# A two-product feed-forward kernel with an order written by hand: high and low parts placed as steps of their own, the written order carried on to the middle of the second product, and four row blocks made in the last unit

## The chip, the cores and the metric

One Trainium2 chip; the program runs on one of its cores. The metric is the device time of one execution in microseconds (us), the median of several runs. The engines of the core are TensorE (PE; its weight loads are listed as PEld), VectorE (DVE), ScalarE (ACT), GpSimd (POOL) and SyncE (SP), which in this kernel issues most DMAs.

## What is computed

One layer of a hybrid trunk over 640 tokens (128 context tokens and 512 latent ones) at a width of 1024: one input projection feeds differential attention, a gated linear recurrence and grouped-query attention, whose outputs are joined and multiplied by `w_out`. A squared-ReLU MLP follows. Cut to the part that matters here, with `g1`, `sh2`, `sc2`, `g2` from the conditioning:

```python
x = LN1(alpha * x + g1 * (mixed @ w_out))          # 640 x 1024
h = x * (1 + sc2) + sh2                            # what the MLP reads
f = square(relu(h @ w_ff1)) @ w_ff2                # 1024 -> 4096 -> 1024
y = LN2(alpha * x + g2 * f)
```

Inputs and outputs are 32-bit floats.

## The kernel before

**Numbers as pairs.** Every large matmul takes its two operands split into a high and a low part. `split` (L90) does it: ScalarE copies the value into the rounded type (the high part, L91), then VectorE subtracts that from the value (the low part, L92). A product is three matmuls, high by high, high by low and low by high (`mm3`, L127, and `prod`, L1417). So an operand is ready only when ScalarE and then VectorE have done their step.

**The output projection** runs in two halves of 512 columns. In each, the five token tiles t (128 tokens) are multiplied in turn (`wo_gemm`, 24 matmuls a tile), VectorE adds the result to the stream (`residual`, L1217; it multiplies by the gate at L1226, which is the reader of the PSUM bank), and takes the statistics (`half_stats`, `norm_stats`). After the second half `normalize` (ScalarE, L1255 to L1258) finishes the tile, `turn` (TensorE, L1268) transposes it in two groups of four blocks, each group into a PSUM bank, and `h2` scales and shifts the group into the MLP's input: the first group by ScalarE (L1281), the second by VectorE (L1279). The input is kept as four quarters `raws[i, j]`: half j of the tokens by half i of the features.

**The first product** (h by `w_ff1`) is made by seven products instead of eight per 2 by 2 block, in 16 units u of 256 hidden columns, two row blocks each. The seven, with their operands, are m1 (a11, b11), m2 (a12, b21), m6 (s2, t2), m5 (s1, t1), m7 (s3, t3), m4 (a22, t4), m3 (s4, b22): 12 matmuls of 320 tokens each. a11, a12 and a22 are quarters of the input, s1 to s4 sums of quarters (`sums12` and its neighbours); the b are quarters of a unit's weights and the t their sums, made by VectorE (`b_sums`, L1300); `load` fetches a unit's weights, and `take` (L1316) splits them: 1 for b11, 2 for b21 and b22, 3 for the four t. In PSUM m1, m6, m7 and m4 add up in bank x, m2 stands in y, m5 and m3 add up in z. `keep` (ScalarE, L1431) copies bank x after m1, m6 and m7, because the next product adds to the same bank and so has to wait for that copy. c11, c22, c12 and c21 (VectorE L1439 to L1444, ScalarE L1436 and L1437) add bank and copy and square the result, and `store` writes a row block to memory through GpSimd's queue, or leaves it in `st` for the last two units. In units 8 to 11 a part of g2 is made as well: `gate2` (L1499) loads weights `wad` into the buffer of a unit's weights, and 8 small matmuls use each half of it at the unit's end.

**The second product** (by `w_ff2`) has two halves n of 512 columns. Its five accumulators take all 32 row blocks in pairs. The blocks of unit 14 come first (`first_pair`, `first_rows`, L1574 and L1620), from weights loaded and split inside the last unit. The loop from L1672 then fetches `wg_i` (512 KB for the blocks i and i+1, two buffers) and reads the stored row blocks `hidb`, splits both, and multiplies; a pair of row blocks is 30 matmuls. In the first half `alpha_rows` (L1655) stands at its tenth block: it loads the rows of LN1's scale and shift, multiplies them by alpha on ScalarE (L1660) and applies them to the stream on VectorE. `gate_rows` (L1207) spreads g2 by two matmuls into `psabg2x` and `psabg2y` (L1213), and ScalarE copies them (L1214).

**What sets the order.** Between `manual_schedule` (after the first half of the output projection) and `region.close()` (after `first_rows`), TensorE, ScalarE and VectorE carry out their instructions as the code writes them. Everything else is ordered by a scheduler. Each engine works through its queue in that order, so a step that waits holds up every step behind it on its engine.

Of the kernel before, what the change touches and what calls it, by code (L numbers as in the profile page):

```python
# [62 lines left out]
def hybrid_layer_kernel(ctx: ExitStack, tc: tile.TileContext, T):  # L63
# [1198 lines left out]
    def turn(t):  # L1262

        for q in range(2):
            pst[t, q] = ps_f(f"psh{t}{q}")
            for k in range(4):
                kk = q * 4 + k
                PE.transpose(pst[t, q][:, k * P : (k + 1) * P], xn[:, t, kk * P : (kk + 1) * P], ident)  # L1268

    def h2(t, q):  # L1270
# [3 lines left out]
        for o, n, th, c0 in spans:  # L1274
# [8 lines left out]
    def split_sum(n, src, lo=0, hi=HALF):  # L1283
        split(sums[n][0][:, :, lo:hi], sums[n][1][:, :, lo:hi], src[:, :, lo:hi])
# [29 lines left out]
    def take(u, what, lo=None, hi=None):  # L1314

        g, o = U[u], u % 2  # L1316
        names, off, src = {
            1: (("b11",), 0, lambda: g.r[:, 0:1, :, 0, :]),
            2: (("b21", "b22"), 2, lambda: g.r[:, 1].rearrange("p k c n -> p c k n")),
            3: (("t1", "t3", "t2", "t4"), 0, lambda: g.t),  # L1320
        }[what]
        lo, hi = lo or 0, hi or len(names)
        if what == 3:
            h, l = f3[o][0][:, lo:hi], f3[o][1][:, lo:hi]
        else:
            n = len(names)
            h, l = f12[o][:, off + lo : off + hi], f12[o][:, off + n + lo : off + n + hi]
        split(h, l, src()[:, lo:hi])
        for i in range(lo, hi):
            g.w[names[i]] = (h[:, i - lo], l[:, i - lo])  # L1330

# [12 lines left out]
    def wo_gemm(t, n, wk):  # L1344
        ps = ps_f(f"pswo{n}{t}")
# [3 lines left out]

    g1r = gate_rows("g1", 0)  # L1350
    wk = wo_weights(0)
    for t in range(NT):
# [16 lines left out]
    for t in range(NT):  # L1369
        ps = wo_gemm(t, 1, wk)  # L1370
        if t == 0:
            g1r = gate_rows("g1", 1)
        if 0 < t < 4:
            turn(t - 1)
        residual(t, 1, ps, g1r, ALPHA)
        half_stats(t, 1, "a")
        mvs[t] = norm_stats(t)
        if t == 4:
            break
        if t > 0:  # L1380
            h2(t - 1, 0)
            h2(t - 1, 1)
        normalize(t, mvs[t])
        if t == 1:
            f3[0] = [wop.tile([P, 4, 4, P], F32R, tag=tag, name=f"wf3{p}0") for p, tag in (("h", "wr"), ("l", "w3"))]
            take(0, 3)
        if t == 2:
            f12 = [mpool[0].tile([P, 6, 4, P], F32R, tag=f"mx{p}", name=f"wf12{p}") for p in "hl"]
            split_sum("a11", raws[0, 0], 0, 256)
            split_sum("a12", raws[0, 1], 0, 256)  # L1390
        if t == 3:
            split_sum("a12", raws[0, 1], 256)
# [22 lines left out]
    def banks(u):  # L1415
        U[u].ps = {b: fps[0].tile([P, 512], F32, tag=b, name=f"ps{b}{u}") for b in "xyz"}
# [96 lines left out]
    m1(0)  # L1513
    turn(3)
    m2(0)
    h2(3, 0)
    take(1, 1)
    h2(3, 1)
# [15 lines left out]
    take(1, 2, 1, 2)
    parts("s1")
    split_sum("s1", s1r)
    m6(1)
    keep(1, 2)
    load(2, wop, "w0")
# [15 lines left out]
    c11(0)  # L1555
    m4(0)
# [233 lines left out]
```

## Time and profile before

| | |
|---|---|
| three runs | 965.54, 967.46, 968.42 us; median 967.46 |
| the profiled execution | 969.56 us, its span 967.8 us |
| mean granted TensorE clock | 0.974 of full speed |
| busy: TensorE, VectorE, ScalarE, GpSimd | 885.0, 664.4, 473.8, 69.0 us |
| bytes moved | 109.19 MB, 113 GB/s over the span |

The profile is one execution. In a row of a timeline stand the start and the duration in us, the engine, the line of the kernel, the operation, what it writes and reads, the tile's shape and the number of instructions; in brackets how long the engine was idle ahead of it and what released it (`<-ACT a L91` means that it waited for the high part that line 91 writes). Matmuls are pipelined, so their starts are what to subtract. The row blocks of a trace's names appear as `hidb`, the parts of the input as `a` and `s`, the weights as `wf12`, `wf3` (their low parts end in l, except where both parts share a buffer), their raw form as `wf_r`, and the sums as `wf_t`.

### The profile page before, as it was taken

The numbers are of one execution on the slowest core, as the hardware profiler recorded it, in microseconds if no ns is written. First come the engines' busy times: TensorE is split into PE (matmuls) and PEld (weight loads), VectorE is DVE, ScalarE is ACT, GpSimd is POOL, SyncE is SP. The second block draws the span as 40 slices with busy tenths as digits, with TensorE's granted clock in tenths as the row PEclk, the third lists the DMA queues.
The fourth block names the chain that finished last, engine by engine and source line by source line (L and its number), as shares of the span: only waits on it lengthen the run. The fifth ranks groups of instructions, "written<-read, shape, count | busy, mean of one in ns | idle before, by whom it ended". The sixth has DMA issues, their size and how long they took to land.

```text
span 967.8 us, 15412 instructions
## 1 busy us (share of the span) xinstructions
PE 885.0 (91%) x5941; PEld 764.0 (79%) x5941; DVE 664.4 (69%) x1231; ACT 473.8 (49%) x972; POOL 69.0 (7%) x136
## 2 busy tenths in 40 slices
PE   6879889999999998999966799999995999999996
PEld 4778776889989776777766799888994888888885
DVE  2369997998786878866756777666754843474448
ACT  3567675476564658632643455444544433153320
POOL 2200010210100100010000000110000000000000
PEclk9999998999999999999979899999997999999998
DMA  9952615423031120053003344455406852052202
GB/s 259 281 154 66 188 37 159 113 83 93 18 99 43 54 90 1 2 204 122 1 1 100 128 142 142 143 172 189 146 28 232 300 175 87 23 174 69 83 11 99
DMA packets 102026, 109.19 MB, mean 113 GB/s; under 512 B 6688, under 2 KB 82176, under 8 KB 101952
## 3 DMA queue, kind: packets, MB, share of 16 engines
q1 hardware_dynamic: 95968, 91.67, 30.6%
q0 software_dynamic: 5792, 16.44, 4.9%
q8 instruction: 47, 0.77, 0.3%
q14 instruction: 27, 0.22, 0.1%
q10 hardware_dynamic: 192, 0.08, 0.0%
HBM read 95.59 MB, written 12.58 MB: 112 GB/s over the span
## 4 chain that ended last, share of the span: by engine, by line
PE 65%; DVE 14%; DMA 9%; ACT 7%; issue 3%; SPq 2%; DVEq 0%; ACTq 0%
PE psx L1425 9%; PE psy L129 7%; PE psy L130 7%; PE psy L131 7%; PE psz L1425 5%; DMA wad<-in_w_ada 3%; PE psA L130 2%; PE psA L129 2%; PE psA L131 2%; PE psavA L731 2%; DMA adaw<-in_w_ada 2%; PE psy L1425 2%; DMA wf_r<-in_w_ff 2%; PE psavC L953 1%; DVE b_st L561 1%
## 5 line engine op out<-in xcount | busy, mean ns | idle before, releaser
L92 DVE TENSOR_TENSOR gl<-hidb,gh 128x640 fp32r<-128x640 f32 x56 | 45.0, 822 | 58.8 <-ACT gh L91 58.8
L91 ACT CAST gh<-hidb 128x640 fp32r<-128x640 f32 x56 | 39.8, 726 | 72.4 <-PE psy L130 65.4
L1425 PE MATMUL psx<-s,wf3h 128*128 128x320 f32 x256 | 60.2, 322 | 9.3 <-ACT s L91 4.9
L129 PE MATMUL psA<-wa_h,xh 128*128 128x384 f32 x160 | 54.8, 344 | 0.0
L131 PE MATMUL psA<-wa_h,xl 128*128 128x384 f32 x160 | 54.4, 341 | 0.0
L130 PE MATMUL psA<-wa_l,xh 128*128 128x384 f32 x160 | 54.2, 340 | 0.0
L1425 PEld LDWEIGHTS psx<-s,wf3h 128*128 128x128 f32 x256 | 45.0, 197 | 10.3 <-ACT s L91 5.1
L1431 ACT COPY kept<-psx 128x320 f32<-128x320 f32 x48 | 20.3, 422 | 63.1 <-PE psx L1425 63.1
L1425 PE MATMUL psx<-s,wf3l 128*128 128x320 f32 x128 | 40.9, 320 | 1.1 <-DVE wf3l L92 1.1
L92 DVE TENSOR_TENSOR wf3l<-wf_t,wf3h 128x2048 fp32r<-128x2048 f32 (+2 forms) x18 | 36.9, 2049 | 5.4 <-ACT wf3h L91 5.4
L91 ACT CAST wf3h<-wf_t 128x2048 fp32r<-128x2048 f32 (+2 forms) x18 | 30.8, 1712 | 3.3 <-DVE wf_t L1310 3.3
L1491 POOL DMA_DIRECT2D hd<-st x28 | 15.3, 546 | 238.5 <-ACT st L1437 138.7
L130 PE MATMUL pswo<-wo,mxh 128*128 128x512 f32 x80 | 31.4, 393 | 0.8 <-DVE wo L92 0.8
L129 PE MATMUL pswo<-wo,mxh 128*128 128x512 f32 x80 | 31.6, 397 | 0.4 <-ACT wo L91 0.4
L1425 PE MATMUL psx<-a,wf3h 128*128 128x320 f32 x128 | 29.6, 318 | 2.4 <-ACT a L91 1.3
L709 DVE TENSOR_REDUCE nmA<-pssA 128x1 f32<-128x768 f32 x32 | 30.2, 951 | 2.2 <-PE pssA L707 1.8
L129 PEld LDWEIGHTS psA<-wa_h,xh 128*128 128x128 f32 x160 | 30.1, 188 | 2.0 <-issue 1.2
L131 PE MATMUL pswo<-wo,mxl 128*128 128x512 f32 x80 | 31.2, 390 | 0.0
L1425 PE MATMUL psz<-s,wf3h 128*128 128x320 f32 x128 | 29.1, 313 | 2.2 <-ACT s L91 1.1
L1444 DVE TENSOR_TENSOR st<-psz,kept 128x320 f32<-128x320 f32 x32 | 15.7, 490 | 22.0 <-PE psz L1425 15.0
L711 ACT ACTIVATE pA<-pssA,nmA 128x768 f32<-128x768 f32 x32 | 28.8, 903 | 3.3 <-DVE nmA L709 2.8
L130 PEld LDWEIGHTS psA<-wa_l,xh 128*128 128x128 f32 x160 | 30.2, 189 | 0.2
(657 smaller groups left out, 2760.0 us busy)
## 6 DMA issues: line engine op xcount, KB each, us to landing
wad<-in_w_ada SPq DMA_DIRECT2D x32, 512.0 KB, 4.7
wf_r<-in_w_ff SPq DMA_DIRECT2D x32, 512.0 KB, 4.1
hd<-st POOLq DMA_DIRECT2D x28, 320.0 KB, 2.5
hidb<-hd SPq DMA_DIRECT2D x28, 320.0 KB, 5.6
adaw<-in_w_ada SPq DMA_DIRECT2D x32, 256.0 KB, 5.3
wa_r<-in_w_in SPq DMA_DIRECT2D x48, 128.0 KB, 2.7
wo_raw<-in_w_out SPq DMA_DIRECT2D x8, 512.0 KB, 6.6
x<-in_x_sample SPq DMA_DIRECT2D x8, 256.0 KB, 4.9
```

The lines of the kernel that those rows point to most:

```text
L91: A.copy(hi, src)
L92: V.tensor_tensor(lo, src, f32(hi), op=ALU.subtract)
L129: PE.matmul(ps, s[0], m[0], start=start, stop=False)
L130: PE.matmul(ps, s[0], m[1], start=False, stop=False)
L131: PE.matmul(ps, s[1], m[0], start=False, stop=stop)
L709: V.tensor_reduce(nm, ps[:, 0:NKEY], axis=AX.X, op=ALU.max, negate=True)
L711: A.activation(pr, ps[:, 0:NKEY], AF.Exp, bias=nm, accum_out=sm[:, col : col + 1])
L731: PE.matmul(po, pT[:, c, :], vals(g, c, c0, n), start=(c == 0), stop=(c == NKC - 1))
L1425: PE.matmul(ps, a_[:, k, :], b_[:, k, :], start=start and k == 0 and i == 0, stop=k == 3 and i == 2, skip_group_check=True)
L1431: A.copy(t, U[u].ps["x"][:, 0:HALF])
L1444: V.tensor_tensor(v, g.ps[b][:, 0:HALF], s, op=ALU.add)
L1491: nc.gpsimd.dma_start(parked[i], t)
```

## The change

1. `take` and `split_sum` fall apart into `hi_` and `lo_` (a unit's weights) and `sum_hi` and `sum_lo` (the input's parts), each placed where the code wants it. b11 of unit 0 is split in the first half of the projection, into a buffer of its own.
2. The start is written anew: b21, b22 and the t of unit 0 are split during the second half of the projection; the PSUM pool is renewed after the projection of tile 3 instead of after tile 4's, so that tile 2's transposes and tile 4's projection already use the new banks (each of x, z, y and f has two); the products of units 0 and 1 come as m1(0), m2(0), m1(1), m2(1), m6(0), m5(0), m6(1), m5(1), m7(0), m7(1), m4(0), m4(1), m3(0), m3(1), with the steps of ScalarE and VectorE between them in a new order.
3. From unit 3 on the high part of b21 and b22 of the next unit stands ahead of c12 of the unit before, no longer behind it.
4. In the last unit the weights for the blocks 0 and 1 and these two blocks are loaded into a buffer of the input (`early`), and split as a second `pair`; all five tiles multiply it right after the first one, and the loop begins with its fifth block.
5. The region closes only after the loop of the second product's first half, and takes in SyncE. `alpha_rows` is cut into steps, one to a row block from the ninth on. The two blocks that were used from `early` are read once more for the second half.

The diff, cut to its core:

```diff
-    def turn(t):
+    def turn(t, bank="f"):
         for q in range(2):
-            pst[t, q] = ps_f(f"psh{t}{q}")
+            pst[t, q] = fps[0].tile([P, 512], F32, tag=bank, name=f"psh{t}{q}")
...
-    region.enter_context(tc.manual_schedule(engines={mybir.EngineType.PE, mybir.EngineType.Activation, mybir.EngineType.DVE}))
+    region.enter_context(tc.manual_schedule(engines={mybir.EngineType.PE, mybir.EngineType.Activation, mybir.EngineType.DVE, mybir.EngineType.SP}))
     wk = wo_weights(1)
     parts("a11", "a12")
     for t in range(NT):
-        ps = wo_gemm(t, 1, wk)
+        ps = wo_gemm(t, 1, wk, "y" if t == 4 else "f")
+        if t == 3:
+            psums.close()
+            fps[0] = psums.enter_context(tc.tile_pool(name="ffps", bufs=2, space=PSUM, reuse_waits="tile"))
+            for b in "xzyf":
+                fps[0].tile([P, 512], F32, tag=b, name=f"ps_{b}")
         if 0 < t < 4:
             turn(t - 1)
+        if t == 2:
+            f12 = [mpool[0].tile([P, 6, 4, P], F32R, tag=f"mx{p}", name=f"wf12{p}") for p in "hl"]
+            hi_(0, 2)
+            lo_(0, 3)
         residual(t, 1, ps, g1r, ALPHA)
...
+        elif t == 2:
+            h2(1, 0)
+            h2(1, 1)
+            sum_hi("a11", raws[0, 0], 0, 256)
+            lo_(0, 2)
+            normalize(2, mvs[2])
+            sum_lo("a11", raws[0, 0], 0, 256)
+            sum_hi("a12", raws[0, 1], 0, 256)
+            sum_lo("a12", raws[0, 1], 0, 256)
...
     c12(0)
-    m3(1)
-    take(2, 2)
     b_sums(2, wop, "w2")
+    hi_(2, 3, 2, 3)
+    lo_(2, 3, 2, 3)
+    hi_(2, 3, 0, 2)
+    lo_(2, 3, 0, 2)
+    hi_(2, 3, 3, 4)
+    lo_(2, 3, 3, 4)
+    hi_(2, 2, 1, 2)
     c12(1)
-    take(2, 3)
+    lo_(2, 2, 1, 2)
...
         m1(u)
+        keep(u, 1)
         if u > 2:
             c22(u - 1)
         if more:
             b_sums(u + 1, wop, "w2")
-            take(u + 1, 1)
+            hi_(u + 1, 1)
+        else:
+            early = sps.tile([P, 1024 + 2 * NTOK], F32, tag="a11", name="early")
+            raw1 = early[:, 0:1024].rearrange("p (k n) -> p k n", n=512)
+            ff2_raw(raw1, 0, 0)
+            for i in range(2):
+                nc.sync.dma_start(early[:, 1024 + i * NTOK : 1024 + (i + 1) * NTOK], parked[i])
         if u > 2:
             m4(u - 1)
             c21(u - 1)
             m3(u - 1)
+        if more:
+            lo_(u + 1, 1)
+            hi_(u + 1, 2)
+            if u > 2:
+                c12(u - 1)
+            lo_(u + 1, 2)
+            hi_(u + 1, 3)
...
         m2(u)
         c11(u)
+        m6(u)
+        keep(u, 2)
         if more:
-            take(u + 1, 3)
+            lo_(u + 1, 3)
             if 8 <= u < 12:
                 gate = gate2(u - 8, f"w{(u + 1) % 2}")
+        else:
+            w1 = wop.tile([P, 4, 512], F32R, tag="w1", name="wg0_p")
+            gs = [wop.tile([P, 2, NTOK], F32R, tag=f"w{i}", name=f"g0_{i}") for i in (2, 0)]
+            pair((w1[:, 0:2], w1[:, 2:4]), *gs, raw1, rows2(early[:, 1024:]))
...
     m3(NU - 1)
     c12(NU - 1)
-    first_rows(2, 3, 4)
-    region.close()
+    for t in range(2, NT):
+        pair_gemm(t, 0)
+    for t in range(NT):
+        pair_gemm(t, 2)
...
-            if n == 0 and m == 9:
-                alpha_rows()
+            if n == 0 and m >= 8:
+                alpha_rows(m - 8)
...
+        if n == 0:
+            for i in range(2):
+                nc.sync.dma_start(hid[i], parked[i])
+            region.close()
         g2r = gate_rows("g2", n, [fps[0].tile([P, 512], F32, tag=b, name=f"psabg2{b}") for b in "xy"] if n == 0 else None)
```

How the order of the instructions moves is seen best in three places. The first is VectorE around the residual of tile 3 in the second half of the projection; `wf12h<-wf_r` of 128x1024 is the low part of unit 0's b21 and b22, `a` are those of a11 and a12, and `pswo` in the last row is tile 3's projection. Before:

```order
L1279 TENSOR_SCALAR q_5121<-psh_5463,a_5030,b_5031 128x128 x4
L92 TENSOR_TENSOR a_5329<-q_5119,a_5329 128x4x256
L92 TENSOR_TENSOR a_5330<-q_5121,a_5330 128x4x256
L1226 TENSOR_TENSOR rt1.18920711500272131_5528<-pswo_5493,g_5356 128x512
L1230 SCALAR_TENSOR_TENSOR xn<-xn,rt1.18920711500272131_5528 128x512
```

and of the changed kernel:

```order
L1279 TENSOR_SCALAR q_5121<-psh_5466,a_5030,b_5031 128x128 x4
L1340 TENSOR_TENSOR wf12h<-wf_r_5178,wf12h 128x1024
L1287 TENSOR_TENSOR a_5333<-q_5119,a_5333 128x4x256
L1287 TENSOR_TENSOR a_5334<-q_5121,a_5334 128x4x256
L1226 TENSOR_TENSOR rt1.18920711500272131_5542<-pswo_5499,g_5360 128x512
L1230 SCALAR_TENSOR_TENSOR xn<-xn,rt1.18920711500272131_5542 128x512
```

A third low part now stands ahead of the instruction that reads the bank, and, by the renewed pool, the second four transposes of tile 2 (`turn`) use that same bank and wait for this L1226; before, they used another one.

The second place is ScalarE in a unit with a gate (unit 9): `kept` are the copies of bank x, the two pairs of ACTIVATE rows are c21 and c12 of the unit before, `wf12h` of 128x1024 is the high part of the next unit's b21 and b22, and `wf3h` that of its sums. Before:

```order
L1431 COPY kept<-psx_6706 128x320
L91 CAST wf12h<-wf_r_6575 128x512
L1436 ACTIVATE st<-psx_6572 128x320
L1437 ACTIVATE st<-st 128x320
L1436 ACTIVATE st<-st 128x320
L1437 ACTIVATE st<-st 128x320
L91 CAST wf12h<-wf_r_6575 128x1024
L91 CAST wf3h_5429<-wf_t_6727 128x2048
```

and of the changed kernel:

```order
L1459 COPY kept<-psx_6712 128x320
L1336 CAST wf12h<-wf_r_6580 128x512
L1464 ACTIVATE st<-psx_6578 128x320
L1465 ACTIVATE st<-st 128x320
L1336 CAST wf12h<-wf_r_6580 128x1024
L1464 ACTIVATE st<-st 128x320
L1465 ACTIVATE st<-st 128x320
L1336 CAST wf3h_5433<-wf_t_6732 128x2048
```

The cast of 128x1024 has moved ahead of the two steps of c12.

The third place is ScalarE where the first product hands over to the second; `ln_g` and `ln_b` are the rows of `alpha_rows`, `gh` the high parts of row blocks, `psabg2x` and `psabg2y` the banks of g2's rows. Before:

```order
L1437 ACTIVATE st<-st 128x320
L1660 ACTIVATE ln_g_7688<-ln_g_7688 128x512
L1660 ACTIVATE ln_g_7689<-ln_g_7689 128x512
L91 CAST gh_7699<-hidb_7664 128x640
L91 CAST gh_7719<-hidb_7665 128x640
L91 CAST gh_7745<-hidb_7666 128x640
L91 CAST gh_7765<-hidb_7667 128x640
L1660 ACTIVATE ln_b_7690<-ln_b_7690 128x512
L91 CAST gh_7791<-hidb_7668 128x640
L1660 ACTIVATE ln_b_7691<-ln_b_7691 128x512
L1214 COPY g_8294<-psabg2x 128x512
L91 CAST wg_0h<-wg_0r 128x1024
```

and of the changed kernel:

```order
L1459 COPY kept<-psx_7461 128x320
L1464 ACTIVATE st<-psx_7461 128x320
L1465 ACTIVATE st<-st 128x320
L1464 ACTIVATE st<-st 128x320
L1465 ACTIVATE st<-st 128x320
L1214 COPY g_8297<-psabg2x 128x512
L1214 COPY g_8300<-psabg2y 128x512
L91 CAST wg_2h<-wg_2r 128x1024
L91 CAST gh_7745<-hidb_7712 128x640
L91 CAST gh_7765<-hidb_7713 128x640
```

The alpha rows have left this place, the casts for the blocks 0 and 1 now lie in the last unit, and both copies of g2's rows stand ahead of the cast of `wg_2`. On TensorE the two matmuls that these copies wait for stand behind the second pair's 30 matmuls, and ahead of the matmuls that read `wg_2`.

More of the change, by code (lines that the diff above doesn't have):

```diff
@@ L1312, in hybrid_layer_kernel, with part @@
     f12, f3 = [None] * 2, [None] * 2
-    def take(u, what, lo=None, hi=None):
+    def part(u, what, lo=None, hi=None):
         g, o = U[u], u % 2
[L1317 to L1321, printed above, removed]
+        names, off = {1: (("b11",), 0), 2: (("b21", "b22"), 2), 3: (("t1", "t3", "t2", "t4"), 0)}[what]
+        src = g.t if what == 3 else g.r[:, 0:1, :, 0, :] if what == 1 else g.r[:, 1].rearrange("p k c n -> p c k n")
         lo, hi = lo or 0, hi or len(names)
@@ L1324, in take @@
             h, l = f3[o][0][:, lo:hi], f3[o][1][:, lo:hi]
+        elif what == 1 and u == 0:
+            h, l = first_b11[:, 0:1], first_b11[:, 1:2]
         else:
@@ L1327, in take, with hi_, lo_ @@
             h, l = f12[o][:, off + lo : off + hi], f12[o][:, off + n + lo : off + n + hi]
-        split(h, l, src()[:, lo:hi])
         for i in range(lo, hi):
             g.w[names[i]] = (h[:, i - lo], l[:, i - lo])
+        return h, l, src[:, lo:hi]
+    def hi_(*a):
+        h, l, src = part(*a)
+        A.copy(h, src)
+    def lo_(*a):
+        h, l, src = part(*a)
+        V.tensor_tensor(l, src, f32(h), op=ALU.subtract)
     def wo_weights(n):
@@ L1342, in wo_weights, with wo_gemm @@
         return out
-    def wo_gemm(t, n, wk):
-        ps = ps_f(f"pswo{n}{t}")
+    def wo_gemm(t, n, wk, bank="f"):
+        ps = fps[0].tile([P, 512], F32, tag=bank, name=f"pswo{n}{t}")
         for k in range(NK):
@@ L1415, in banks @@
     def banks(u):
[L1416 removed]
+        U[u].ps = {b: fps[0].tile([P, 512], F32, tag=b, name=f"ps{b}{u}") for b in "xy"}
     def prod(u, b, sn, wn, start):
@@ L1457, in m5 @@
     def m5(u):
+        U[u].ps["z"] = fps[0].tile([P, 512], F32, tag="z", name=f"psz{u}")
         prod(u, "z", "s1", "t1", True)
@@ L1513, in hybrid_layer_kernel @@
     m1(0)
+    keep(0, 1)
+    h2(2, 0, 1)
+    lo_(1, 1)
+    h2(2, 1, 1)
+    m2(0)
     turn(3)
[L1515 to L1518, printed above, removed]
     normalize(4, mvs[4])
     m1(1)
-    turn(4)
-    take(1, 2, 0, 1)
+    turn(4, "z")
+    h2(3, 1)
+    lo_(1, 2, 0, 1)
+    m2(1)
+    h2(3, 0)
+    keep(1, 1)
     sums12(0, 192)
-    m2(1)
-    take(1, 3, 2, 3)
     h2(4, 0)
     h2(4, 1)
+    hi_(1, 3, 2, 3)
     parts("s2")
-    split_sum("s2", s2r, 0, 192)
+    sum_hi("s2", s2r, 0, 192)
+    hi_(1, 3, 0, 2)
     sums12(192, HALF)
-    split_sum("s2", s2r, 192)
+    sum_lo("s2", s2r, 0, 192)
+    sum_hi("s2", s2r, 192)
+    sum_lo("s2", s2r, 192)
+    parts("s1")
+    sum_hi("s1", s1r)
+    sum_lo("s1", s1r)
+    load(2, wop, "w0")
+    lo_(1, 3, 2, 3)
+    hi_(1, 3, 3, 4)
+    hi_(1, 2, 1, 2)
     m6(0)
     keep(0, 2)
[L1534 to L1539, printed above, removed]
     m5(0)
@@ L1555, in hybrid_layer_kernel @@
     c11(0)
+    sum_hi("s4", s2r)
+    sum_lo("s4", s2r)
+    load(3, wop, "w1")
+    keep(1, 3)
     m4(0)
-    split_sum("s4", s2r)
-    load(3, wop, "w1")
+    m4(1)
     c21(0)
```

158 lines of the change are left out of this document (84 added, 74 removed).

## The prediction

> **What bounds the kernel now.** The profiled execution took 969.56 us, of which the span is 967.8; the median of the three timed runs is 967.46. I made the sum against the profiled execution and moved it down by the difference, 2.10 us. The page gives TensorE 885.0 us of work, 91% of the span, and 65% of the chain of waits. So the question is not which engine bounds the kernel but where TensorE still stops. The windows of 20 us answer it (bounds and length, then the busy time of TensorE, its weight loads, VectorE, ScalarE and GpSimd, the granted clock, and the DMA share and rate). From the end of the output projection, about 480 us, they read
>
> ```profile
> 480.00:500.00 20.00, 14.90 (x78) 12.63 (x77) 15.13 (x36) 12.50 (x29) 0.00 (x0) 0.91 0.00 1
> 500.00:520.00 20.00, 13.80 (x72) 12.37 (x72) 10.28 (x11) 7.53 (x11) 0.00 (x0) 0.83 0.16 52
> 520.00:540.00 20.00, 13.13 (x72) 12.15 (x72) 13.20 (x18) 6.90 (x13) 1.64 (x3) 0.91 0.32 103
> 540.00:560.00 20.00, 16.57 (x97) 16.10 (x98) 15.19 (x17) 11.05 (x16) 1.62 (x3) 0.83 0.43 147
> 560.00:580.00 20.00, 20.00 (x138) 20.00 (x138) 15.78 (x21) 9.31 (x17) 1.08 (x2) 1.00 0.46 146
> 720.00:740.00 20.00, 14.99 (x85) 13.32 (x83) 5.74 (x9) 4.68 (x10) 2.13 (x4) 0.98 0.58 198
> 740.00:760.00 20.00, 14.41 (x56) 11.65 (x56) 18.68 (x27) 13.81 (x20) 0.00 (x0) 0.76 0.63 210
> ```
>
> Three stretches are left: the start of the first product (480 to 560, TensorE busy 58 of 80 us, at a granted clock of 0.83 to 0.91), small losses in units 8 to 11, and the hand-over to the second product (720 to 760). Outside them TensorE is busy without a gap, as in 560 to 580, and nothing that shortens another engine can gain there. TensorE's timeline names the holes of the start:
>
> ```profile
> 482.77 0.39 PE L131 MATMUL pswo<-wo,mxl 128*128 128x512 f32 x1
> 485.54 0.56 PE L1425 MATMUL psx<-a,wf12h 128*128 128x320 f32 x2 [2.38 <-ACT wf12h L91]
> 502.81 1.36 PE L1425 MATMUL psx<-s,wf3h 128*128 128x320 f32 x2 [4.86 <-ACT s L91]
> 526.84 2.94 PE L1425 MATMUL psz<-s,wf12h 128*128 128x320 f32 x12 [2.83 <-DVE st L1444]
> 531.97 1.92 PE L1425 MATMUL psz<-s,wf12l 128*128 128x320 f32 x12
> 533.73 1.92 PE L1425 MATMUL psx<-a,wf12h 128*128 128x320 f32 x12
> 558.20 0.45 PE L1425 MATMUL psx<-s,wf3h 128*128 128x320 f32 x2
> ```
>
> A product of 12 matmuls takes 533.73 - 531.97 = 1.76 us at full speed. Each hole costs more than its length: the 24 matmuls from 526.84 to 531.97 took 5.13 us where two products take 3.52, 1.61 lost after a hole of 2.83. The granted clock shows why:
>
> ```profile
> 488.00:490.00 2.00, 2.00 (x10) 1.96 (x10) 1.20 (x4) 0.49 (x2) 0.00 (x0) 0.50 0.00 0
> ```
>
> This is half clock after a hole of 2.38. I price a hole of 2.3 us or more at its length and 1.85 us of slow clock, somewhat above those 1.61 since the slow stretch may last longer.
>
> [...]
>
> **The start, 23 products, steps apart.** The diff places high and low parts singly and puts most of the third and fourth turned tiles' work after several products. I walked the new order in before's clock. Up to 476.5 nothing changes. Then there is a new wait. The pool of PSUM banks is renewed one tile earlier, so the second four transposes of tile 2 now land in the bank that holds tile 3's projection and have to wait until residual(3) has read it. On VectorE residual(3) stands behind three low parts:
>
> ```profile
> 477.54 2.36 DVE L92 TENSOR_TENSOR a<-q,a 128x1024 fp32r<-128x1024 f32 x2 [1.74 <-ACT a L91]
> 479.82 0.68 DVE L1226 TENSOR_TENSOR 1.18920711500272131_5528<-pswo,g 128x512 f32<-128x512 f32 x1
> 476.55 1.10 PE L1268 MATMUL psh<-ident,xn 128*128 128x128 f32 x8 [0.27 <-ACT xn L1258]
> ```
>
> The added low part (128x1024, half of 2.36, so 1.18) fits where VectorE idles 1.74, so residual(3) comes at 479.83 as before. But TensorE used to run on from 477.41 and now stands from 477.05 (half of its eight transposes) to 479.87: 2.8 us and 1.85 of slow clock. What is queued behind is the whole of tile 4's projection: four transposes 0.5, 24 matmuls at 0.227 (30 of them take 6.80, rows below) 5.4, so its end moves from 483.16 to 487.7. From there m1(0), m2(0), turn 3, m1(1), turn 4 and m2(1) follow without a hole (the parts they read are made meanwhile): four products 7.0, two turns 2.0, 0.2 of waits, to 496.9. The 2.38 at 485.54 is gone, since those parts are ready by 485.5.
>
> Then m6(0) needs s2, whose last part needs tile 4. On ScalarE stand behind turn 4 (ended 495.05):
>
> ```profile
> 495.35 0.62 ACT L91 CAST wf3h<-wf_t 128x512 fp32r<-128x512 f32 x1
> 495.87 1.51 ACT L1281 ACTIVATE q<-psh,b,a 128x128 f32<-128x128 f32 x4
> 498.07 0.83 ACT L91 CAST s<-s2r 128x768 fp32r<-128x768 f32 x1 [0.70 <-DVE s2r L1509]
> 634.71 1.03 ACT L91 CAST wf12h<-wf_r 128x1024 fp32r<-128x1024 f32 x1
> ```
>
> the copy 1.51, casts 0.62, 0.83, 1.03 and s2's last 0.62: 4.6, so 499.75, and the low part 0.7 later. Hole 2.9 + 0.7, where there were 4.86. With 1.85 of slow clock, twelve products (m6(0) to m2(2)) 21.1 and 0.7 they end at 523.4; the holes up to 526.84 go, as each operand is now made a product or more ahead. Next m6(2) waits for keep(2,1). In ScalarE's order that copy stands behind the casts of unit 2's sums and c12(1), whose sum on VectorE follows b_sums(2) and those casts' low parts:
>
> ```profile
> 536.08 1.22 DVE L1308 TENSOR_TENSOR wf_t<-wf_r 128x1024 f32<-128x1024 f32 x1
> 537.34 0.69 DVE L1309 TENSOR_TENSOR wf_t<-wf_r,wf_t 128x512 f32<-128x512 f32 x1
> 538.67 0.48 DVE L1444 TENSOR_TENSOR st<-psz,kept 128x320 f32<-128x320 f32 x1
> ```
>
> From 518.6 (m3(0) ended 518.1, c12(0)'s sum 0.48): 1.22 + 0.69 + 0.69, the first cast 0.62, low parts 0.62 + 1.22 + 0.68, sum 0.48, c12(1)'s two 0.47 on ScalarE, the copy 0.4: 526.6. Hole 3.2. Seven products and slow clock 1.85 bring m2(3) to 540.8, say 541.0, where before had 558.20. **Gain 17.2.** If the bank's wait does not bite it is 21; one more hole of 2.4 with its slow clock leaves 13.
>
> **Units 8 to 11.** The hidden gate's weights are loaded into a buffer that is free when the low part of b21 and b22 is done.
>
> ```profile
> L144 PE MATMUL psadag<-wad,cs 128*32 128x256 f32 x64 | 5.1, 390 | 5.2 <-DMA wad<-in_w_ada 5.2
> 640.86 0.64 PE L144 MATMUL psadag<-wad,cs 128*32 128x256 f32 x8 [0.55 <-DMA wad<-in_w_ada]
> 642.64 0.64 PE L144 MATMUL psadag<-wad,cs 128*32 128x256 f32 x8 [1.14 <-DMA wad<-in_w_ada]
> 646.25 0.74 PE L1425 MATMUL psx<-a,wf3h 128*128 128x320 f32 x2
> 633.31 0.49 DVE L1444 TENSOR_TENSOR st<-psz,kept 128x320 f32<-128x320 f32 x1
> 635.78 1.23 DVE L92 TENSOR_TENSOR wf12h<-wf_r,wf12h 128x1024 fp32r<-128x1024 f32 x1 [1.98 <-ACT wf12h L91]
> ```
>
> The cast (634.71) stood behind both steps of c12; now it stands ahead of them. It still waits until m3 has read the old weights (TensorE done at 633.3, when VectorE's sum starts), so it begins at 633.3 and the low part at 634.33 instead of 635.78: loads 1.45 earlier. The second of the four gates lost 0.55 + 1.14 = 1.69, the others 3.5 together, 1.2 each; so 5.2 shrinks to 0.24. After the second gate two matmuls took 0.74 where 0.45 is usual (as at 558.20); I put that slow stretch at 1.5, near the start's, and it goes too. **Gain 6.5** (4 if the loads land no more than 1 us earlier, 7 at most). c12 ends about 1 us later for it; its store is read only in the second product, so that costs nothing.
>
> **The hand-over.** The second product's first pair of row blocks was multiplied before; then TensorE waited 10.60 us, because ScalarE stood 6.25 us at the multiply of ln1's rows, with the casts behind it:
>
> ```profile
> 738.21 0.63 ACT L1660 ACTIVATE ln_g<-ln_g 128x512 f32<-128x512 f32 x1 [6.25 <-DMA ln_g<-in_ln_g]
> 744.03 0.56 ACT L1214 COPY g<-psabg2x 128x512 f32<-128x512 f32 x1
> 744.49 1.04 ACT L91 CAST wg_0h<-wg_0r 128x1024 fp32r<-128x1024 f32 x1
> 745.59 1.65 PE L129 MATMUL psy<-wg_0h,gh 128*128 128x512 f32 x3 [10.60 <-ACT wg_0h L91]
> 754.33 0.39 PE L129 MATMUL psy<-wg_2h,gh 128*128 128x512 f32 x1
> 761.13 0.39 PE L129 MATMUL psy<-wg_4h,gh 128*128 128x512 f32 x1
> ```
>
> A pair is 30 matmuls, 761.13 - 754.33 = 6.80 at full speed, and 8.74 after the hole. Now the pair (0,1) is split inside the last unit and follows at once: from 734.37 to 741.17. Then the fixed order strikes: the two gate matmuls (0.46) end at 741.63, and ScalarE's two copies of them stand ahead of the cast of wg_2, whose data landed long ago. Two copies at 0.46, the cast 0.95, a row block's 0.7: TensorE goes on at 744.25, a hole of 2.6, and that pair, like the first one before, takes 8.74: done at 753.0. It ended at 761.13. **Gain 8.0.** If those copies did not block, 741.63 + 6.80 gives 12.7; if wg_2 is late by 3 us as well, 5. The rows of ln1, spread one step to a row block, add about 1.4 to VectorE and nothing to TensorE.
>
> Early splitting of b11 in the first half of the projection (a cast 0.62, a low part 0.7) lies in stretches where both engines idle: 0, at most 1.
>
> **Sum:** 17.2 + 6.5 + 8.0 = 31.7; 969.56 - 31.7 = 937.9; less 2.10, about 936.
>
> **Rivals.** *More (0.15).* The bank's wait or the copies cost less: with a start of 21, the gates and 12.7, 40.2 are gained: 927. If only the clock stayed up over the holes of 2.8 and 2.6, 3.7 more: 932. Against the clock's staying up: 2.38 halved it. [...]
>
> *Less (0.18).* The fixed order puts single steps of ScalarE and VectorE in one line, so one late step delays all behind it; the start then gains 8 instead of 17 (two further holes of 2.4 with 1.85 each): 945.
>
> *It doesn't do what it says (0.06).* The early pair isn't ready: its rows are loaded when a11's buffer is free, after m1(15). If so the hand-over keeps its hole and gains 1: 943. Against it: from m1(15) to the pair TensorE has a unit of seven products (12.3) and a pair (6.8), 19.1 us, and a landing of 8.7 with the splits of a pair, 5.35 (rows below), takes 14.0.
>
> *Slower (0.04).* SyncE is in the fixed order too. A fetch of w_ff2 waits for the low part two pairs back, and blocks the row blocks' reads behind it. Its round is landing, cast 1.03, low 1.23, and two row blocks' casts and lows, for two buffers:
>
> ```profile
> L92 DVE TENSOR_TENSOR gl<-hidb,gh 128x640 fp32r<-128x640 f32 x56 | 45.0, 822 | 58.8 <-ACT gh L91 58.8
> L91 ACT CAST gh<-hidb 128x640 fp32r<-128x640 f32 x56 | 39.8, 726 | 72.4 <-PE psy L130 65.4
> wg_0r<-in_w_ff SPq DMA_DIRECT2D x2, 512.0 KB, 8.7
> ```
>
> (landing + 5.35) / 2: 7.0 us at the longest landing, 8.7, against 6.80, a loss of 0.2 x 14 pairs. It decides only above 9.1 us a pair (14 x 2.3 eats the 31.7), a landing of 12.8; at 14.5 the kernel takes about 980. No row is near.
>
> **Chances.** Forecast 0.55. A measurement can tell about 0.3%, 2.9 us. The first three rivals are faster by more, so faster 0.94; slower 0.04; 0.02 for the slower case just eating the gain. The bounds 13 + 4 + 5 = 22 and 40.7 give 945.5 and 926.8: range 926 to 947.
>
> **What would show it.** Right: TensorE idle about 2.8 us inside tile 2's transposes, released by VectorE's L1226; unit 3's m2 ended near 541; no row over 0.3 at the gate matmuls but in unit 9; after psabg2y a hole near 2.6 released by ScalarE's cast of wg_2. Wrong: a hole before the second product as long as before, gate rows as before, or gaps between pairs in the second product.

## The result, and the profile after

The changed kernel takes 940.90 us (median of four runs, 940.01 to 943.91), the kernel before 966.50 (four runs, 963.87 to 968.42). The ratio is 0.974, with a 95% interval of 0.971 to 0.978: 25.6 us faster, where 31.5 had been forecast (936). The profiled execution after took 940.01 us, span 938.2; before it was 969.56 and 967.8.

To see where it came from, four marks of TensorE's timeline cut both profiles: the first transposes of tile 2, the start of unit 3's m6 (the end of its m2), the end of m3(15), and the first matmul of the block pair (4, 5) in the second product.

| stretch, us | before | after | gained | forecast |
|---|---|---|---|---|
| up to tile 2's transposes | 476.55 | 475.34 | 1.2 | 0 |
| start: to unit 3's m6 | 81.65 | 63.28 | 18.4 | 17.2 |
| units 3 to 15: to the end of m3(15) | 172.06 | 169.60 | 2.5 | 6.5 |
| hand-over: to the pair (4, 5) | 30.87 | 23.50 | 7.4 | 8.0 |
| rest | 206.67 | 206.48 | 0.2 | 0 |

The 1.2 us ahead of the change are not its work: in the profiles of the runs below, of which none edits that part, this mark lies between 474.57 and 478.84. The two profiled executions differ by 29.6 us and the medians by 25.6, since the one before lies above every timed run of its kernel given here and the one after is the fastest of its four; the stretches together show some 4 us too much. Of 31.7 us, one term of 6.5 came out as 2.5; the others were within 1.2.

Five rows of TensorE's timeline after, from tile 2's transposes to unit 3's m6 (in brackets the hole and what ended it). Three of them have a hole of over 0.3 us, and there is no other one in that stretch:

```profile
478.64 1.11 PE L1268 MATMUL psh<-ident,xn 128*128 128x128 f32 x4 [2.64 <-DVE 1.18920711500272131_5542 L1226]
485.88 1.92 PE L1453 MATMUL psx<-a,b 128*128 128x320 f32 x12
498.41 0.63 PE L1453 MATMUL psx<-s,wf3h 128*128 128x320 f32 x1 [2.97 <-ACT s L1284]
524.66 0.56 PE L1453 MATMUL psx<-s,wf3h 128*128 128x320 f32 x2 [3.02 <-ACT kept L1459]
538.62 0.46 PE L1453 MATMUL psx<-s,wf3h 128*128 128x320 f32 x2
```

They are the three holes of the walk: the new one in tile 2's transposes, released by L1226 (2.8 forecast), m6(0) waiting for s2 (2.9), m6(2) waiting for keep(2,1) (3.2); m1(0) at 485.88 has none, and unit 3's m6 stands at 538.62 where 541.0 was forecast and 558.20 measured before. The windows that answer to those shown of before:

```profile
480.00:500.00 20.00, 16.60 (x92) 14.45 (x91) 14.59 (x35) 14.66 (x32) 0.00 (x0) 0.93 0.01 1
500.00:520.00 20.00, 20.00 (x132) 20.00 (x131) 18.72 (x24) 10.20 (x19) 1.64 (x3) 0.95 0.43 139
520.00:540.00 20.00, 16.98 (x106) 16.72 (x105) 17.55 (x24) 12.36 (x20) 1.62 (x3) 0.91 0.46 153
540.00:560.00 20.00, 20.00 (x138) 20.00 (x137) 14.47 (x18) 8.79 (x16) 1.08 (x2) 1.00 0.46 156
700.00:720.00 20.00, 19.76 (x101) 16.93 (x99) 5.06 (x8) 3.90 (x8) 2.13 (x4) 1.00 0.48 167
720.00:740.00 20.00, 17.38 (x67) 13.76 (x68) 14.39 (x17) 15.93 (x23) 0.00 (x0) 0.91 0.78 283
```

From 480 to 560 TensorE is busy 73.6 of 80 us, where it was 58.4. The hand-over, on TensorE and then on ScalarE:

```profile
719.36 0.40 PE L1213 MATMUL psabg2y<-grows,sel 128*128 128x512 f32 x1
722.25 0.50 PE L129 MATMUL psy<-wg_2h,gh 128*128 128x512 f32 x1 [2.50 <-ACT gh L91]
731.72 0.39 PE L129 MATMUL psy<-wg_4h,gh 128*128 128x512 f32 x1
```
```profile
719.56 0.59 ACT L1214 COPY g<-psabg2x 128x512 f32<-128x512 f32 x1 [9.64 <-PE psabg2x L1213]
720.04 0.59 ACT L1214 COPY g<-psabg2y 128x512 f32<-128x512 f32 x1
720.52 1.06 ACT L91 CAST wg_2h<-wg_2r 128x1024 fp32r<-128x1024 f32 x1
```

ScalarE stood 9.64 us at the copies; the cast of wg_2 came right behind them, and TensorE's hole is 2.50 (2.6 forecast).

The gates are what went otherwise. The group of their matmuls (count, busy time and mean, idle time ahead of them):

```profile
L144 PE MATMUL psadag<-wad,cs 128*32 128x256 f32 x64 | 5.1, 390 | 4.4 <-DMA wad<-in_w_ada 4.4
```

The timelines in unit 9: ScalarE's cast and c12's first step, SyncE's loads of the gate's weights, GpSimd's store of c12, and TensorE at the gate:

```profile
612.97 1.05 ACT L1336 CAST wf12h<-wf_r 128x1024 fp32r<-128x1024 f32 x1 [0.67 <-PE psz L1453]
613.92 0.47 ACT L1464 ACTIVATE st<-st 128x320 f32<-128x320 f32 x1
615.30 1.75 SPq L1526 DMA_DIRECT2D wad<-in_w_ada  x2
615.18 0.56 POOL L1518 DMA_DIRECT2D hd<-st  x1 [2.02 <-ACT st L1465]
621.14 0.64 PE L144 MATMUL psadag<-wad,cs 128*32 128x256 f32 x8 [1.02 <-DMA wad<-in_w_ada]
622.59 0.64 PE L144 MATMUL psadag<-wad,cs 128*32 128x256 f32 x8 [0.81 <-DMA wad<-in_w_ada]
```

The cast did move ahead of c12, and the loads are issued 2.19 us behind the start of VectorE's sum of c12 (613.11), where it was 3.72 before (633.31): 1.53 us earlier in the unit, as forecast. But the gates wait 4.4 us together, not 0.24. The store of c12's row block (320 KB) starts 0.12 us ahead of the loads (1 MB). Before, it stood 1.93 us ahead of them:

```profile
635.10 0.56 POOL L1491 DMA_DIRECT2D hd<-st  x1 [1.74 <-ACT st L1437]
637.03 0.92 SPq L1499 DMA_DIRECT2D wad<-in_w_ada  x2
```

The median time from a load's issue to its landing in these four units rose from 3.7 to 5.4 us. So two theories stood for that term: the store that slid into the loads takes the DMA engines from them; or the loads are slower in this phase of the unit for a reason of their own. For the other terms the runs ask whether each hole has the cause that the walk gave it, and which part of the hand-over's change did the work.

### The profile page after: what moved, and what is told of

Its sections match the earlier page's. It is cut to its first block, busy times and chain, and to the rows that moved or that the text cites. A ratio compares the mean times of both kernels' runs of the same rounds, so it can differ in the third digit from the quotient of the medians.

```text
span 938.2 us, 15408 instructions
## 1 busy us (share of the span) xinstructions
PE 880.3 (94%) x5941; PEld 762.6 (81%) x5941; DVE 665.1 (71%) x1232; ACT 474.9 (51%) x973; POOL 69.0 (7%) x136
## 4 chain that ended last, share of the span: by engine, by line
PE 67%; DVE 15%; DMA 8%; ACT 6%; issue 3%; SPq 1%; DVEq 0%; ACTq 0%
PE psx L1453 10%; PE psy L131 8%; PE psy L129 8%; PE psy L130 8%; PE psz L1453 5%; DMA wad<-in_w_ada 3%; PE psA L130 2%; PE psA L129 2%; PE psA L131 2%; PE psavA L731 2%; DVE b_st L561 2%; PE psy L1453 2%; DMA wf_r<-in_w_ff 2%; PE psavC L953 1%; DVE b_lqk L516 1%
## 5 line engine op out<-in xcount | busy, mean ns | idle before, releaser
L130 PE MATMUL pswo<-wo,mxh 128*128 128x512 f32 x80 | 31.7, 397 | 0.8 <-DVE wo L92 0.8
L131 PE MATMUL pswo<-wo,mxl 128*128 128x512 f32 x80 | 31.5, 393 | 0.0
L131 PEld LDWEIGHTS psA<-wa_h,xl 128*128 128x128 f32 x160 | 30.1, 188 | 0.2
```

Source lines behind the costliest of these rows:

```text
L130: PE.matmul(ps, s[0], m[1], start=False, stop=False)
L131: PE.matmul(ps, s[1], m[0], start=False, stop=stop)
```

## The experiments

All are edits of the changed kernel. The base, run again on the chip of the first group:

> The changed kernel once more, as the base for the other runs of this chip. 940 to 943 us, the gate matmuls waiting some 4.4 us together, holes of TensorE near 2.6, 3.0, 3.0 and 2.5 us.

Measured: 941.87 us (six runs, 940.46 to 946.12), ratio to the kernel before 0.974 (0.972 to 0.976). Its profile (span 938.7): start 63.31, units 169.08, hand-over 23.49, gate waits 3.9. The runs of one kernel scatter by 1 to 7 us, and the later runs are from two other chips, so below the ratios to the kernel before, which ran on each of the chips, stand beside the stretches.

**The gates.** First the store behind the loads:

```diff
-                c12(u - 1)
+                c12(u - 1, not 8 <= u < 12)
...
                 gate = gate2(u - 8, f"w{(u + 1) % 2}")
+                store(u - 1, 1, nc.sync)
```

(the new argument of `c12` leaves the store to the added line, that of `store` names the queue)

> The changed kernel, but in the units 8 to 11 c12's row block is written to memory through SyncE's queue, behind the two loads of the gate's weights, instead of through GpSimd's queue as soon as it is made. Theory (the store, which now starts together with the loads because c12 comes later, takes the DMA engines from them for about 0.9 us a unit): each pair of loads lands in 5.0 to 5.3 us instead of 6.1 to 6.6, the gates' waits fall from 4.4 to about 0.5 to 1.0 us, and the time by 3.5 us. Rival (the loads land later for a reason of their own, since they are issued in another phase of the unit): waits stay at 4 us or more and the time within 1 us of the base.

Measured: 937.62 us, ratio 0.969 (0.967 to 0.972), 4.3 us under the base by the medians; of this the two profiles show 2.2 (units 166.90 us, in the base 169.08). The group of the gates' matmuls:

```profile
L144 PE MATMUL psadag<-wad,cs 128*32 128x256 f32 x64 | 5.1, 391 | 1.9 <-DMA wad<-in_w_ada 1.7
```

TensorE's timeline at the gates of units 8, 9 and 10:

```profile
607.77 0.64 PE L144 MATMUL psadag<-wad,cs 128*32 128x256 f32 x8 [0.24 <-DMA wad<-in_w_ada]
622.99 0.64 PE L144 MATMUL psadag<-wad,cs 128*32 128x256 f32 x8 [1.49 <-DMA wad<-in_w_ada]
636.08 1.37 PE L144 MATMUL psadag<-wad,cs 128*32 128x256 f32 x16
```

In units 10 and 11 nothing waits any more, in unit 8 only 0.24; unit 9 keeps 1.49. The waits stay above the 0.5 to 1.0 us of the theory because of unit 9 alone. The median landing is 4.6, but it is taken over another mix: the trace has a landing for six of the eight loads, and the second load of a pair takes longer than the first. Counted apart, the first loads land in 3.7 to 4.1 us (in the changed kernel 4.6 to 5.8, before 3.5 to 3.8), and the second ones in 5.0, in unit 9 in 6.4 (in the changed kernel 5.7 and 6.8, before 4.7 and 5.2). So with the store out of the way, and the loads in the same phase of the unit, most of the delay is gone. Then the opposite, c12 ahead of the cast again, the rest as changed:

```diff
             lo_(u + 1, 1)
-            hi_(u + 1, 2)
             if u > 2:
                 c12(u - 1)
+            hi_(u + 1, 2)
             lo_(u + 1, 2)
```

> The changed kernel with one move undone: from unit 3 on c12 of the unit before stands ahead of the high part of b21 and b22 again. Theory (the move issues the loads 1.45 us earlier, and the store gives most of it back): the loads are issued 1.4 to 1.5 us later in the unit but land in 5.0 to 5.2 us again; the waits are 5 to 5.5 us where the base has 4.4, with 1.5 us of slow clock more if one wait passes 1.6 us; 1 to 2.5 us slower than the base. Rival (the loads' later landing has nothing to do with c12): they land in 6.1 to 6.6 us as in the base, the waits rise to about 10 us and the time by 6 us or more.

Measured: 942.61 us, ratio 0.975 (0.972 to 0.978), not to be told from the base. The group of the gates' matmuls:

```profile
L144 PE MATMUL psadag<-wad,cs 128*32 128x256 f32 x64 | 5.1, 390 | 4.8 <-DMA wad<-in_w_ada 4.8
```

The store and the loads in unit 9:

```profile
621.73 0.56 POOL L1518 DMA_DIRECT2D hd<-st  x1 [1.74 <-ACT st L1465]
623.66 1.00 SPq L1526 DMA_DIRECT2D wad<-in_w_ada  x2
```

The store is 1.93 us ahead again, the median landing is 3.7 again, and the waits are 4.8, just under the theory's 5 to 5.5; the 1 to 2.5 us of time that it gave can't be told from the scatter. The rival of the first run asked for waits of 4 us or more, that of the second for slow landings and about 10 us of waits; both fell. The second run puts the loads back as well as the store, so it is the first that tells the store from the phase of the unit; the second shows that the same store through GpSimd's queue costs the loads nothing when it starts 1.93 us ahead. The move as built is worth 0.4 to 0.9 us of waits, and with the store out of the way 3.1 (4.8 to 1.7); unit 9 keeps the rest.

**The bank.**

```diff
-            pst[t, q] = fps[0].tile([P, 512], F32, tag=bank, name=f"psh{t}{q}")
+            pst[t, q] = fps[0].tile([P, 512], F32, tag="z" if (t, q) == (2, 1) else bank, name=f"psh{t}{q}")
```

> The changed kernel, but the second four transposes of tile 2 go to a bank of z that has long been read, not to the one that holds tile 3's projection. Theory (that bank is the whole reason of the 2.64 us hole, and its slow clock comes with it): the hole goes, tile 4's projection ends 4 to 4.5 us earlier, and most of that reaches m6(0), since its operands hang on tile 4: 3.5 to 4.5 us faster than the base. Rival (the hole only moves): what m6(0) waits for is bound by ScalarE's and VectorE's work on tiles 2 and 3, so the hole ahead of m6(0) grows from 3.0 to 6 or 7 us, and the time stays within 1 us of the base.

Measured: 936.30 us, ratio 0.968 (0.965 to 0.970), 5.6 us under the base by the medians. TensorE, and ScalarE's cast that m6(0) waits for:

```profile
474.57 1.10 PE L1268 MATMUL psh<-ident,xn 128*128 128x128 f32 x8 [0.27 <-ACT xn L1258]
493.77 0.64 PE L1453 MATMUL psx<-s,wf3h 128*128 128x320 f32 x1 [3.59 <-ACT s L1284]
493.10 0.62 ACT L1284 CAST s<-s2r 128x512 fp32r<-128x512 f32 x1 [0.91 <-DVE s2r L1536]
```

All eight transposes run on, and m6(0) follows 19.20 us after them, in the base 499.36 - 476.27 = 23.09: 3.9 us less, while m6(0)'s own hole grew only from 2.97 to 3.59. The rival fell. The start as a whole shortened only from 63.31 to 60.56 in this profile: behind m6(0)'s hole the half clock lasted 6.83 us, in the base 3.41, so that there is as much of it in both although one hole is gone. The timed runs gained more than that one profile shows.

**The hand-over.** g2's rows ahead of m3(15):

```diff
     pair_gemm(1, 0)
+    g20 = gate_rows("g2", 0, [fps[0].tile([P, 512], F32, tag=b, name=f"psabg2{b}") for b in "xy"])
     m3(NU - 1)
...
-        g2r = gate_rows("g2", n, [fps[0].tile([P, 512], F32, tag=b, name=f"psabg2{b}") for b in "xy"] if n == 0 else None)
+        g2r = g20 if n == 0 else gate_rows("g2", n)
```

> The changed kernel, but the two matmuls that spread g2 and ScalarE's two copies of them stand ahead of the last product m3(15), not behind the second pair. Theory (the two copies, which wait for TensorE to end the pair, hold back the casts of wg_2, and nothing else does): ScalarE casts wg_2 while TensorE multiplies the second pair, the hole of 2.5 us and the slow clock behind it go, 4.4 to 4.7 us faster than the base. Rival (the weights and row blocks of wg_2 land late): the cast of wg_2 then waits for a DMA and the hole stays at 1.5 us or more.

Measured: 936.67 us, ratio 0.969 (0.966 to 0.971); hand-over 17.73 us instead of 23.5 (0.46 of this are g2's two matmuls, which now stand ahead of the mark). TensorE begins wg_2 without a hole:

```profile
723.89 0.39 PE L129 MATMUL psy<-wg_2h,gh 128*128 128x512 f32 x1
```

So the two copies were all that held TensorE, and wg_2's data came in time (it landed in 3.6 us). Next, the second early pair taken out (its buffer `early`, its loads, its split and its `pair_gemm`; the loop begins with block 0):

> The changed kernel without its second early pair: the last unit makes two row blocks as before, the loop begins with blocks 0 and 1, all else stays (SyncE and the second product's first half in the written order, the alpha rows spread). Theory (the second pair covers the landing of the first fetch, 6.8 us): TensorE stops for 5 to 7.5 us behind the first pair, until wg_0 has landed and is split, then runs a pair at slow clock; 2.5 to 4.5 us slower than the base. Rival (what mattered was that the alpha rows left this place, and the pair adds nothing): a hole of 3 us or less, and within 1 us of the base.

Measured: 943.03 us, ratio 0.975 (0.972 to 0.978), not to be told from the base; hand-over 23.46, the base's 23.49. SyncE's fetch, ScalarE's copy, TensorE:

```profile
711.14 0.37 SPq L1748 DMA_DIRECT2D wg_0r<-in_w_ff  x1
715.46 0.59 ACT L1214 COPY g<-psabg2x 128x512 f32<-128x512 f32 x1 [2.81 <-PE psabg2x L1213]
718.53 0.50 PE L129 MATMUL psy<-wg_0h,gh 128*128 128x512 f32 x1 [2.87 <-ACT gh L91]
```

Here the rival was right: the second pair adds nothing to the kernel as built. wg_0 lands in 3.6 us, by 714.7, before ScalarE gets to the copies; with one pair or two, TensorE stops once, 2.87 or 2.50 us, at those copies. Is the pair worth nothing, or do the copies hide its worth? Both edits together, g2's rows early and one pair:

> The run with g2's rows early, and without the second early pair. In the run with one pair alone the hole ahead of the loop was 2.87 us against 2.50 with two, since both waited for the copies of g2's rows. Theory (the second pair covers the first fetch of the loop, about 3.6 us of landing and 2.5 of splitting, and only the copies hid that): with the copies gone the lack of the pair shows, a hole of 3 to 4 us and slow clock, and the stretch from m3(15) to the third pair of the loop takes 22 to 23.5 us where two pairs take 17.7. Rival (the second pair covers nothing): 17.7 to 19 us.

Measured: 941.20 us, ratio 0.973 (0.969 to 0.976); hand-over 23.31 us, with two pairs 17.73. TensorE's first matmul of the loop:

```profile
719.04 0.50 PE L129 MATMUL psy<-wg_0h,gh 128*128 128x512 f32 x1 [3.28 <-ACT gh L91]
```

The pair is worth 5.6 us once nothing else stops TensorE at that place. And what did gain the 7.4? The alpha rows put back ahead of the loop, with one pair:

```diff
+    alpha_rows(0)
+    alpha_rows(4)
     ws, gs = itertools.count(), itertools.count()
...
-            if n == 0 and m >= 8:
+            if n == 0 and m > 12:
```

> The run with one early pair, but ScalarE multiplies all four of LN1's rows by alpha right ahead of the loop, as the kernel before did, instead of at the loop's thirteenth block. Theory (the gain of the hand-over comes from these rows leaving this place): ScalarE waits for their load, which lands 7 to 9 us after m3(15), so TensorE's hole grows from 2.9 to 6 us or more, and the stretch from m3(15) to the third pair from 23.5 to 27 us or more; 4 us or more slower than the run with one pair. Rival (the rows land in time, and it was the order of the casts that mattered): the stretch stays at 23 to 25 us.

Measured: 948.68 us, ratio 0.981 (0.979 to 0.984); hand-over 30.02, without this edit 23.46, in the kernel before 30.87. ScalarE and TensorE:

```profile
717.22 0.63 ACT L1724 ACTIVATE ln_g<-ln_g 128x512 f32<-128x512 f32 x1 [4.57 <-DMA ln_g<-in_ln_g]
724.17 0.80 PE L129 MATMUL psy<-wg_0h,gh 128*128 128x512 f32 x1 [8.48 <-ACT gh L91]
```

Most of the hole of the kernel before is back, 8.48 of 10.60 us, and ScalarE waits for the load of ln_g as it did there. Moving four small multiplies away from the hand-over is worth 6.6 us with one pair, of the 7.4 that it gained.

**The hole ahead of m6(2).**

```diff
-    c12(1)
     lo_(2, 2, 1, 2)
...
         keep(u, 1)
+        if u == 2:
+            c12(1)
```

> The changed kernel, but c12 of unit 1 comes after keep(2,1), so that ScalarE copies bank x before it waits for that sum. Theory (the copy stands behind a step that isn't needed yet): the hole of 3.0 us ahead of m6(2) shrinks to 1.5 us or less, and with the slow clock behind it 3 to 4.5 us are gained. Rival (ScalarE is held just as long by the casts of unit 2's sums, which wait for VectorE): the hole stays above 2.4 us, slow clock included, and the gain is under 1 us.

Measured: 941.37 us, ratio 0.974 (0.971 to 0.976): nothing gained. TensorE at m6(2) and m7(2):

```profile
522.84 0.56 PE L1453 MATMUL psx<-s,wf3h 128*128 128x320 f32 x2 [0.79 <-ACT kept L1459]
529.19 0.56 PE L1453 MATMUL psx<-s,wf3h 128*128 128x320 f32 x2 [2.56 <-ACT kept L1459]
```

Neither theory had it: the hole at m6(2) shrank as the first said, and the rest came back two products later at the next copy, which stands on ScalarE behind the same c12(1) and unit 3's casts. I then took VectorE's work for the bound of this stretch, and moved 2 us of it to ScalarE, on top of this edit (the same in c22):

```diff
     def c11(u):
-        out_sum(u, "y", U[u].s1, 0, 0, False)
+        out_sum(u, "y", U[u].s1, 0, 0, u < 2)
```

> The run with keep(2,1) first, and the squared ReLU of c11 and c22 of units 0 and 1 on ScalarE (two steps of 0.47 us) instead of VectorE (one of 0.49). In the run before this one the hole ahead of unit 2 only moved, 3.0 us to 0.8 + 2.6, and VectorE worked without a pause from 499 to 532. Theory (VectorE's work bounds this stretch): 2.0 us less of it shorten the two holes to 1.5 us or less together, and the time by 1.5 to 3.5 us. Rival (a chain of waits between the engines bounds it, whatever VectorE does): holes of 3 us or more together.

Measured: 940.81 us, ratio 0.973 (0.971 to 0.976). TensorE:

```profile
515.14 0.56 PE L1453 MATMUL psx<-a,wf3h 128*128 128x320 f32 x2 [0.45 <-ACT kept L1459]
530.68 0.58 PE L1453 MATMUL psx<-s,wf3h 128*128 128x320 f32 x2 [2.56 <-ACT kept L1459]
```

The same 2.56 us at m7(2), and a new 0.45 at m4(0): 3.01 together, as the rival had it, and no gain in time. But VectorE had not worked without a pause in the run before (it idled 0.81 and 0.40 us), and the work that was taken off it lies ahead of its sum for c12(0). That sum now waits 0.28 us for TensorE's m3(0), so the relief ended there. Behind it VectorE works through unit 2's sums, the low parts and c12(1)'s sum with one pause of 0.26 us (518.97 to 525.78), and then ScalarE through c12(1), three casts and the copy that m7(2) waits for (525.82 to 530.63). So a chain of waits from TensorE through both engines bounds this place; whether less work on VectorE behind that sum would help, and which link would have to go first, stays open.

**Together.** All four edits, and then with c11 and c22 of the first units on ScalarE as well:

> All four edits at once on the changed kernel: the store behind the gate's loads, the other bank for tile 2, g2's rows early, keep(2,1) ahead of c12 of unit 1. If each hole is its own, the gains add up: 3.5 + 4 + 4.5 + 3.5, about 15 us under the base, near 926 us. If what one gives the next takes (the start's edits share VectorE and ScalarE), 8 to 11 us.

> All four edits, and the squared ReLU of units 0 and 1 on ScalarE. If VectorE bounds the start, 1.5 to 3.5 us under the run with all four edits (928.9), so 925.4 to 927.4; if a chain of waits does, within 1 us of it.

Measured: 928.88 us, ratio 0.960 (0.958 to 0.962), and 930.32, ratio 0.962 (0.960 to 0.965). By the ratios the four edits took 0.45, 0.64, 0.54 and 0.02% off the base one by one, 1.65% in sum, and 1.35% together: additive within the intervals. The first of the two is 13 us under the base, between the two cases of its expectation. The second is no faster: its start takes 59.93 us in the profile, that of the first 60.13.

## Why the prediction was right, and where it was not

*The start* (17.2, measured 18.4). Each of the three holes came where the order put it, with its releaser, and within 0.2 us of its size; the extra wait for s2's low part was 0.19 and not 0.7. The bank's wait, priced at 3.8 (21 against 17.2), cost 3.9 up to m6(0). The hole ahead of m6(0) had been walked along ScalarE; with the other bank ScalarE itself idles 0.91 us there for VectorE's s2, so VectorE's chain ended last in that run, and the sum came out by two chains of nearly one length. The hole at m6(2) came in its place with 3.02 us; the terms written out for it add up to 526.2, not 526.6, so to a hole of 2.8 and not 3.2, and it hung on more than the steps that were named. That the total came so near is luck in part: in this stretch the trace before has six steps of 3.41 us at half clock and the one after three, each worth up to 1.7 us (last section), and their number changes from one execution to the next.

*The slow clock*, 1.85 us behind each hole of 2.3 or more, did follow each of the four holes of the trace after, but its size varies: from tile 2's second transposes to the second half of turn 3, the same work, the base took 11.8 us and the run with c12 first 13.2. The clock was halved there for one such step in the base, for two in the other.

*The gates* (6.5, measured 2.5: 0.8 of waits and the rest from the slow stretch that is gone behind the second gate). This is the step that failed: "loads 1.45 earlier" was taken for landings 1.45 earlier, and beside it stood "c12 ends about 1 us later for it; its store is read only in the second product, so that costs nothing". The loads were issued earlier by as much as that; but only the reader of the store was looked at, and not what its transfer does to loads that start beside it. The median landing went from 3.7 to 5.4 us. The run with the store behind the loads shows the cause, and the one with c12 first agrees with it.

*The hand-over* (8.0, measured 7.4). Hole and copies came as walked; the slow pair took 9.47 us (722.25 to 731.72) and not 8.74. But the text let the second pair carry the gain ("now the pair (0,1) is split inside the last unit and follows at once"). In the kernel as built it carried none of it, since the copies stopped TensorE with it or without it; the size was right, the part that was credited with it was not. What gained was the departure of the alpha rows, which the prediction named as the cause of the old hole and did not price by itself. The landing of 8.7 us of wg_0, of which the case of the unready pair made use, was 3.6 here.

*The rivals.* The slower case didn't come near: from 740 to 920 TensorE is busy in every window of 20 us without a gap, and the rest took 206.48 us, before 206.67. The case of a larger gain described what two edits then did (the bank, g2's rows), and the one of a smaller gain did not come, since the start gained 18.4; but the line of waits that it feared is what the hole at m6(2) hangs on, which only moves when it is pushed.

## What to carry to other kernels

When a step is moved later "for nothing", follow its DMA too: ask what else will be on the DMA engines at the moment at which it now starts, not only who reads its result (here the store came 0.12 instead of 1.93 us ahead of the loads, and their median landing took 5.4 us instead of 3.7). A cover such as the second pair is worth nothing while another wait at the same place ends later (hand-over 23.49 us with it and 23.46 without; with the copies out of the way 17.73 and 23.31); find out which wait ends last with and without it, and test the two apart and together. In a written order a hole that is taken away at one copy can come back at the next if both stand behind the same chain, as the 3.01 us ahead of m6(2) did: 0.79 there and 2.56 ahead of m7(2).

## What the runs showed of the hardware

Behind the holes of 2.38 us or more at the start and at the hand-over the half clock came as a rule, but not always at once, and not always. In the base, after the hole of 3.01 us, TensorE's rows read:

```profile
525.62 0.55 PE L1453 MATMUL psx<-s,wf3h 128*128 128x320 f32 x2 [3.01 <-ACT kept L1459]
527.28 0.73 PE L1453 MATMUL psx<-s,wf3h 128*128 128x320 f32 x2
530.33 0.45 PE L1453 MATMUL psz<-s,wf3h 128*128 128x320 f32 x2
```

Full speed for 1 us, half speed for some 3, then full again; with the other bank the same product was slow from its first matmul at 521.45. The granted clock's own record shows it. In every profile its changes lie on a grid of 3.41 us (in the kernel before the half clock begins at 486.60, 500.25, 527.56, 541.22 and 643.62, always a whole number of steps apart; with the other bank at 520.86, within the hole), and up to 10 us before the end it lasts one to four whole steps (3.41 to 10.24 us in the kernel before, 3.41 to 13.65 in the changed one). In these profiles it went with how long TensorE was busy, by the profile's records, within the step before. The steps around that hole in the base, and then around the same hole of 2.56 us ahead of m7(2) in the two runs with all four edits (bounds, length, TensorE's busy time, granted clock, DMA share and rate):

```profile
523.30:526.71 3.41, 1.09 (x7) 1.00 0.18 32
526.71:530.13 3.42, 3.42 (x15) 0.50 1.03 349
```
```profile
521.75:525.16 3.41, 0.85 (x6) 1.00 0.87 311
525.16:528.57 3.41, 3.41 (x15) 0.50 0.95 302
```
```profile
523.48:526.89 3.41, 2.28 (x16) 1.00 0.80 248
526.89:530.31 3.42, 1.98 (x13) 1.00 0.78 257
530.31:533.72 3.41, 3.41 (x26) 1.00 0.60 206
```

In the last run (the one with c11 and c22 on ScalarE) the hole falls across the border of two steps, TensorE is busy over half of each (2.28 and 1.98 us), and the clock stays up. Over all fourteen profiles, from the first record of the clock to 10 us before the end, half clock followed on all 81 steps at full clock in which TensorE was busy under 45%, on 20 of the 27 with 45 to 55%, and on one of the 3458 with more (in the profiles before and after: 13 of 13, 3 of 5, none of 497). So here a hole cost its length and, by where it fell on the grid, nothing more or up to 1.7 us (half of 3.41) for each step at half clock. Half clock followed holes of 2.38, 2.50 and 2.64 us, and in the kernel before even the gate's waits of 0.55 and 1.14 us, with TensorE busy 1.72 us of the step that ended at 643.62.

In unit 9, and in no other of the four, SyncE took 0.89 to 1.59 us to issue the gate's second load in all twelve profiles in which c12 comes later, and 0.51 to 0.59 in the kernel before and with c12 first. The second load landed late there with the store behind it too; why is open.
